# Attention of a hybrid trunk layer: scores of the next group of queries ahead of a group's products, shorter filling, a third P buffer for a weight buffer

## The chip, the cores and the metric

The kernel runs on one core of a Trainium2 chip. The metric is the device time of one execution in microseconds (us). A core has a matrix engine (PE), whose weight loads are listed apart (PEld), a vector engine (DVE), an activation engine (ACT), GpSimd (POOL), and SP, which here only issues DMAs. PE accumulates in PSUM, and the vector and activation engines read results from there.

## What is computed

Two trunk layers over 640 tokens of width 1024 (512 latent tokens, then 128 prompt tokens). Each layer normalises its input, projects it, runs three branches side by side (gated linear attention, latent attention with 4 heads, a diagonal state space model called S5), merges them by sigmoid gates, and projects out. The change is in the attention branch.

```python
def block_attention(q, k, v):
    ...
    def one_block(q_blk):
        s = jnp.einsum('bhqd,bhkd->bhqk', q_blk, k).astype(jnp.float32) * scale
        p = jax.nn.softmax(s, axis=-1).astype(v.dtype)
        return jnp.einsum('bhqk,bhkd->bhqd', p, v)
...
    mixed = (g_a * ((o_a * jax.nn.silu(g_gate)) @ p['w_bo_gla'])
             + g_b * ((o_b * jax.nn.silu(m_gate)) @ p['w_bo_mla'])
             + g_c * ((o_c * jax.nn.silu(s_gate)) @ p['w_bo_s5']))
    y = x + gate * (mixed @ p['w_out'])
```

Latent queries see 256 cached and 512 latent keys (6 blocks of 128); prompt queries see the 128 prompt keys alone.

## The kernel before

Values are split into a rounded high part and the rest (`whi`/`wlo`, `vh`/`vl`, `Pth`/`Ptl`), and a product is the sum of three matmuls. Weights arrive by DMA in raw tiles `wraw` of 128x512, of which there are 4; ACT copies the high part (L227) and DVE subtracts (L236). The order on PE is the order of the code; a scheduler sets the order on the other engines.

The heads (`mla_heads`, L1169) run one after the other. A head has three groups of queries: A and B with two blocks of 128 queries against 768 keys, C with one block against 128 keys. For a block, PE writes scores into two PSUM banks of 128x384 (one for C), DVE finds the maximum of each bank (`tensor_reduce`, L1211), joins and negates them, ACT computes two exponentials from the banks into `P` with the row sums, and DVE adds the sums, takes the reciprocal and scales `P`. `out` (L1228) then turns `P` around on PE (transposes, L1236), in three pieces that are split into `Pth` and `Ptl`, and multiplies each with the values; DVE multiplies the result with a gate into `og` (L1253). `load(h+1)` transposes the next head's queries and keys into single-buffered tiles; `values(h+1)` splits the next head's values into `vh` and `vl`.

The tag `bank` has 4 PSUM banks, shared by scores, transposes, products and loads.

To cover chains on ACT and DVE, `fill(n)` puts n steps of other work on PE, taken from a list of generators, `stand`. One step is mostly six 128x320 matmuls of a projection. In the heads that list holds the merging of the S5 branch, alternating with the modulation of this layer (`ada`, which holds one of the 4 banks until it is done and reads `wraw` directly, two tiles a step), and then early gate tiles of another branch (`mer_early`). `FM` says how many steps stand where: by its places, ahead of A's scores, ahead of A's products, after each piece of products, after B's scores, ahead of B's products, between A's two blocks, between B's two blocks, within C, and within `load`. When the list is empty `fill` puts nothing. Gate tiles not started in the heads are computed in `merge(0, ...)`, near the layer's end, instead of being read back.

Of the kernel before, what the change touches and what calls it, by code (L numbers as in the profile page):

```python
# [10 lines left out]
F32 = mybir.dt.float32  # L11
# [3 lines left out]
AF = mybir.ActivationFunctionType  # L15
ALU = mybir.AluOpType
AX = mybir.AxisListType
# [165 lines left out]


FILL = (17, 2, 1, 4, 2, 10, 10, 1, 7, 3)
FM = (1, 6, 1, 4, 2, 4, 3, 2, 1)
FG = (7, 2, 2, 5, 5)
TCARGS = dict(schedule_with_timeline_sim=True)
OUTS = {"yT": (8, 128, NT), "ckvo": (L, 2, 128, NP_), "kro": (L, 32, NP_), "glao": (L, 4, 128, 128), "s5o": (L, 128, 64)}
# [12 lines left out]
class Prog:  # L202
# [59 lines left out]
        return hi, lo  # L262

    def raw(self, l, name, i):
        r = self.wp.tile([128, 512], F32, name="wraw", tag="wraw", bufs=4)
        self.S.dma_start(r, self.a["wpk"][l, self.at[name]][:, 512 * i:512 * i + 512])
        return r

# [900 lines left out]
    def mla_heads(self, p):  # L1169
        V, fill = self.V, self.fill  # L1170
        scale = 96.0 ** -0.5
        mk = lambda nm, n, b: p.tile([128, n], F32R, name=nm, tag=nm, bufs=b)

        A, B, C = (0, 256, 0, 6), (256, 256, 0, 6), (512, 128, 6, 1)

        def load(h):

            q, k = (mk("qTh", NT, 1), mk("qTl", NT, 1)), (mk("kTh", 896, 1), mk("kTl", 896, 1))
            for src, tiles, d, c0 in ((self.qt, range(0, 4), q, 0), (self.kt, range(0, 4), k, 0),
                                      (self.kt, range(4, 7), k, 512), (self.qt, range(4, 5), q, 512)):  # L1180
                ps = self.bank()
                for i, t in enumerate(tiles):
                    self.T.transpose(ps[0:96, 128 * i:128 * i + 128], src[:, t, h, :], self.ident)
                n = 128 * len(tiles)
                self.split(d[0][0:96, c0:c0 + n], d[1][0:96, c0:c0 + n], ps[0:96, 0:n])
                if c0 == 0 and d is k:
                    fill(FM[8])
            return q, k

        def values(h):  # L1190
            v = [p.tile([128, 7, 128], F32R, name=nm, tag=nm, bufs=1) for nm in ("vh", "vl")]
            self.split(v[0], v[1], self.vt[:, :, 128 * h:128 * h + 128])
            return v

        def scores(qk, grp, n):

            q0, nq, k0, nk = grp
            q, k = qk
            pr = []
            for qi in range(nq // 128):  # L1200
                fill(n * qi)
                qc = slice(q0 + 128 * qi, q0 + 128 * qi + 128)
                P = p.tile([128, 768], F32, name="P", tag="P", bufs=2) if nk > 1 else p.tile([128, 128], F32, name="Pp", tag="Pp")
                mx = p.tile([128, 4], F32, name="smx", tag="smx", bufs=3)
                parts = [(0, 384), (384, 384)] if nk == 6 else [(0, 128)]
                pss = []
                for i, (c0, w) in enumerate(parts):
                    ps = self.bank()
                    kc = slice(128 * k0 + c0, 128 * k0 + c0 + w)
                    self.mm3([ps[:, 0:w]], (q[0][0:96, qc], q[1][0:96, qc]), (k[0][0:96], k[1][0:96]), [kc], True, True)  # L1210
                    V.tensor_reduce(mx[:, i:i + 1], ps[:, 0:w], axis=AX.X, op=ALU.max)  # L1211
                    pss.append(ps)
                if len(parts) == 2:
                    V.tensor_tensor(mx[:, 0:1], mx[:, 0:1], mx[:, 1:2], op=ALU.max)
                V.tensor_scalar(mx[:, 0:1], mx[:, 0:1], -scale, None, op0=ALU.mult)  # L1215
                for i, (c0, w) in enumerate(parts):
                    self.act(P[:, c0:c0 + w], pss[i][:, 0:w], AF.Exp, scale=scale, bias=mx[:, 0:1],
                             accum_out=mx[:, 2 + i:3 + i])
                if len(parts) == 2:
                    V.tensor_tensor(mx[:, 2:3], mx[:, 2:3], mx[:, 3:4], op=ALU.add)  # L1220
                V.reciprocal(mx[:, 2:3], mx[:, 2:3])
                V.tensor_scalar(P[:, 0:128 * nk], P[:, 0:128 * nk], mx[:, 2:3], 0.5, op0=ALU.mult, op1=ALU.mult)
                pr.append(P)
            return pr

        def out(h, pr, v, grp, og, g):
            q0, nq, k0, nk = grp
            po = self.bank()  # L1228
            todo = []
            for k2 in range(0, nk, 2):  # L1230
                ks = range(k2, min(k2 + 2, nk))
                pt = self.bank()
                n = nq * len(ks)
                for i, k in enumerate(ks):
                    for qi in range(nq // 128):
                        self.T.transpose(pt[:, nq * i + 128 * qi:nq * i + 128 * qi + 128], pr[qi][:, 128 * k:128 * k + 128], self.ident)  # L1236
                if nk == 1:
                    th, tl = p.tile([128, 128], F32, name="Pt", tag="Pt", bufs=2), None
                    self.copy(th, pt[:, 0:n])
                else:  # L1240
                    th, tl = mk("Pth", 512, 2), mk("Ptl", 512, 2)
                    self.split(th[:, 0:n], tl[:, 0:n], pt[:, 0:n])
                todo.append((ks, th, tl))
                if len(todo) == 2:
                    yield
                    self.pv(po, v, todo.pop(0), grp)
            yield
            if nk == 1:
                self.mm(po[:, 0:nq], self.vt[:, k0, 128 * h:128 * h + 128], todo[0][1])
            else:  # L1250
                self.pv(po, v, todo.pop(0), grp)
            c = slice(q0, q0 + nq)
            V.tensor_tensor(og[:, c], po[:, 0:nq], g[:, c], op=ALU.mult)  # L1253

        qk, v = load(0), None
        ogs = []
        for h in range(4):
            og = self.ogp.tile([128, NT], F32, name="og", tag="og", bufs=12)
            g = self.gate_in(h)
            fill(FM[0])  # L1260
            pr = scores(qk, A, FM[5])
            if not h:
                v = values(0)
            fill(FM[1])
            for _ in out(h, pr, v, A, og, g):
                fill(FM[2])
            pr = scores(qk, B, FM[6])
            fill(FM[3])
            prc = scores(qk, C, 0)
            if h < 3:  # L1270
                qk = load(h + 1)
            fill(FM[4])
            for _ in out(h, pr, v, B, og, g):
                fill(FM[2])
            for _ in out(h, prc, v, C, og, g):
                fill(FM[7])
            if h < 3:
                v = values(h + 1)
            ogs.append(og)
        return ogs  # L1280
# [10 lines left out]
    def gla_in(self, pa, p):  # L1291
        V, l = self.V, self.l
        self.gq, self.gk = [], []
        for name, dst, s in (("gq", self.gq, 0.125), ("gk", self.gk, 1.0)):
            for i in range(2):
# [3 lines left out]
                dst.append(t)  # L1299
        raw = p.tile([96, 512], F32, name="wa2")  # L1300
        self.S.dma_start(raw, self.a["wa2"][l])
        wa = p.tile([96, 512], F32R, name="wa3")
        self.copy(wa, raw)
        V.tensor_tensor(wa[32:64], raw[32:64], wa[32:64].bitcast(F32), op=ALU.subtract)
        ba = p.tile([128, 512], F32, name="ba")
# [140 lines left out]
    def fill(self, n):  # L1446

        for _ in range(n):
            while self.stand:
                try:  # L1450
                    next(self.stand[0])
                    break
                except StopIteration:
                    self.stand.pop(0)
# [179 lines left out]
```

## Time and profile before

| | |
|---|---|
| time, median of 3 runs | 1606.06 us (1602.31 to 1606.08) |
| profiled execution | 1601.22 us, span 1599.4 us |
| mean granted PE clock | 0.981 |
| busy: PE, DVE, ACT | 95%, 66%, 40% of the span |
| heads of the first layer | about 396 to 540 us of the span |
| heads of the second layer | end at 1328.6 us |

Times in the rows below are us from the span's start. A number in square brackets at a row's end is how long the engine stood idle before that row's first instruction, and what released it.

### The profile page before, as it was taken

What the parts mean: (1) busy time and instruction counts of PE and PEld (TensorE: products, weight loads), DVE (VectorE), ACT (ScalarE), POOL (GpSimd) and SP (SyncE); (2) the same over time, 40 slices, a digit from 0 to 9 for tenths busy, and PEclk for the clock granted to TensorE, in tenths of its full rate; (3) what the DMA queues carried; (4) which work ended last, traced back from release to release, by engine and by line L of the source; (5) the groups of instructions that cost most, each with busy time, mean ns of one, the idle gap of its engine ahead of it and who ended that gap; (6) DMA issues with size and microseconds to landing.
All of it is one profiled execution on the core that took longest, in us unless ns stands there. A gap on an engine that the chain in (4) does not pass through costs nothing. (4 is left out here: it accounts for less than half of the span.)

```text
span 1599.4 us, 28779 instructions
## 1 busy us (share of the span) xinstructions
PE 1516.4 (95%) x11334; PEld 1438.9 (90%) x11334; DVE 1056.4 (66%) x2435; ACT 631.8 (40%) x1171; POOL 47.7 (3%) x48
## 2 busy tenths in 40 slices
PE   4999999999998898999799999999999989989999
PEld 3789999999997888898697999999999979889998
DVE  8986992367566436879987579724766663477762
ACT  3335223555444353333223542244544442634331
POOL 0000000012000000000000000000210000000000
PEclk9999999999999899999899999999999999999999
DMA  9451435323311121227553432442332122212253
GB/s 339 169 152 42 154 114 157 117 86 115 113 55 58 46 75 54 65 85 255 206 193 92 124 112 90 138 151 76 106 120 93 55 66 66 68 60 60 93 166 107
DMA packets 108792, 179.73 MB, mean 112 GB/s; under 512 B 12656, under 2 KB 30768, under 8 KB 108656
## 3 DMA queue, kind: packets, MB, share of 16 engines
q1 hardware_dynamic: 108656, 177.89, 34.3%
q8 instruction: 89, 1.46, 0.4%
q14 instruction: 47, 0.39, 0.1%
HBM read 149.23 MB, written 28.61 MB: 111 GB/s over the span
## 5 line engine op out<-in xcount | busy, mean ns | idle before, releaser
L245 PE MATMUL pj<-h,whi 128*128 128x320 f32 x3456 | 664.1, 313 | 0.0
L245 PEld LDWEIGHTS pj<-h,whi 128*128 128x128 f32 x3456 | 541.2, 189 | 6.6 <-issue 5.1
L227 ACT ACTIVATE whi<-wraw 128x512 fp32r<-128x512 f32 x326 | 205.0, 631 | 508.4 <-PE pj L245 359.2
L245 PE MATMUL pj<-h,wlo 128*128 128x320 f32 x1728 | 397.3, 310 | 0.0
L236 DVE TENSOR_TENSOR wlo<-wraw,whi 128x512 fp32r<-128x512 f32 x326 | 223.9, 688 | 245.5 <-ACT whi L227 238.6
L245 PEld LDWEIGHTS pj<-h,wlo 128*128 128x128 f32 x1728 | 290.3, 188 | 0.0
L245 PE MATMUL pj<-og,whi 128*128 128x320 f32 x736 | 142.1, 313 | 0.3 <-DVE og L236 0.3
L245 PEld LDWEIGHTS pj<-og,whi 128*128 128x128 f32 x736 | 114.7, 188 | 4.7 <-ACT whi L227 1.6
L245 PE MATMUL pj<-whi,h 128*128 128x512 f32 x256 | 87.1, 401 | 6.3 <-ACT h L230 5.7
L245 PE MATMUL pj<-og,wlo 128*128 128x320 f32 x384 | 87.5, 309 | 0.0
L245 PEld LDWEIGHTS pj<-whi,h 128*128 128x128 f32 x256 | 48.7, 192 | 19.5 <-ACT h L230 6.3
L245 PEld LDWEIGHTS pj<-og,wlo 128*128 128x128 f32 x384 | 64.2, 188 | 0.0
L230 ACT ACTIVATE P<-bank,smx 128x384 f32<-128x384 f32 x64 | 36.4, 575 | 56.0 <-DVE smx L1215 56.0
L236 DVE TENSOR_TENSOR Ptl<-bank,Pth 128x512 fp32r<-128x512 f32 x48 | 32.1, 689 | 34.3 <-ACT Pth L227 33.7
L230 ACT ACTIVATE th<-pj 128x640 f32<-128x640 f32 x72 | 49.6, 689 | 5.5 <-PE pj L245 5.4
L245 PE MATMUL pj<-wlo,h 128*128 128x512 f32 x128 | 50.8, 397 | 0.0
L245 PE MATMUL pj<-s5g,whi 128*128 128x320 f32 x256 | 48.1, 310 | 0.0
L245 PE MATMUL bank<-s5qy,mx 128*80 128x128 f32 x256 | 46.1, 302 | 0.0
L227 ACT ACTIVATE Pth<-bank 128x512 fp32r<-128x512 f32 x48 | 27.5, 596 | 41.3 <-PE bank L1236 41.1
L1236 PE MATMUL bank<-c,P 128*128 128x128 f32 x192 | 32.2, 304 | 11.9 <-ACT P L230 5.3
L1211 DVE TENSOR_REDUCE smx<-bank 128x1 f32<-128x384 f32 (+1 forms) x72 | 36.2, 524 | 9.0 <-PE bank L245 8.1
L1400 DVE SCALAR_TENSOR_TENSOR st<-st,bl,bank 64x128 f32<-64x128 f32 x112 | 38.9, 347 | 3.6
(349 smaller groups left out, 2324.2 us busy)
## 6 DMA issues: line engine op xcount, KB each, us to landing
wraw<-wpk SPq DMA_DIRECT2D x358, 256.0 KB, 2.7
og<-wpk SPq DMA_DIRECT2D x48, 256.0 KB, 5.1
qd<-s5qk SPq DMA_DIRECT2D x32, 256.0 KB, 2.2
s5qy<-qd SPq DMA_DIRECT2D x32, 256.0 KB, 4.1
gd<-gt SPq DMA_DIRECT2D x16, 320.0 KB, 2.5
gt<-gd SPq DMA_DIRECT2D x16, 320.0 KB, 3.1
md<-th SPq DMA_DIRECT2D x16, 320.0 KB, 2.3
th<-md SPq DMA_DIRECT2D x16, 320.0 KB, 3.1
```

Source lines behind the costliest of these rows:

```text
L227: self.A.activation(out, in_, AF.Copy, scale=scale)
L230: self.A.activation(out, in_, f, **kw)
L236: (eng or self.V).tensor_tensor(lo, src, hi.bitcast(F32), op=ALU.subtract)
L245: self.T.matmul(out, lhsT, rhs, start=start, stop=stop, skip_group_check=True, **kw)
L1211: V.tensor_reduce(mx[:, i:i + 1], ps[:, 0:w], axis=AX.X, op=ALU.max)
L1236: self.T.transpose(pt[:, nq * i + 128 * qi:nq * i + 128 * qi + 128], pr[qi][:, 128 * k:128 * k + 128], self.ident)
L1400: V.scalar_tensor_tensor(out, st[r, c, :], bl[r, c:c + 1], pu[c][r], op0=ALU.mult, op1=ALU.add)
```

## The change

The function for a group's scores becomes one for a single block of queries, and the loop over heads is written in another order: A's scores of the first head come ahead of the loop; B's first block comes ahead of A's products; B's second block and C come after A's products; and A's two blocks of the next head come ahead of C's product. No filling stands between two blocks of one group. A head without `load` asks for 28 filling steps before and 13 now (4, three times 1, 2, three times 1, 1); `load` adds one in both. `P` gets a third buffer of 128x768, and `wraw` loses one of four.

```diff
-FM = (1, 6, 1, 4, 2, 4, 3, 2, 1)
+FM = (1, 4, 1, 2, 1, 0, 0, 0, 1)
...
-        r = self.wp.tile([128, 512], F32, name="wraw", tag="wraw", bufs=4)
+        r = self.wp.tile([128, 512], F32, name="wraw", tag="wraw", bufs=3)
...
-        def scores(qk, grp, n):
+        def score(qk, grp, qi):
...
-            for qi in range(nq // 128):
-                fill(n * qi)
...
-                P = p.tile([128, 768], F32, name="P", tag="P", bufs=2) if nk > 1 else p.tile([128, 128], F32, name="Pp", tag="Pp")
+            P = p.tile([128, 768], F32, name="P", tag="P", bufs=3) if nk > 1 else p.tile([128, 128], F32, name="Pp", tag="Pp")
...
-        qk, v = load(0), None
+        qk = load(0)
+        fill(FM[0])
+        pa = [score(qk, A, 0), score(qk, A, 1)]
+        v = values(0)
...
-            fill(FM[0])
-            pr = scores(qk, A, FM[5])
-            if not h:
-                v = values(0)
+            pb = [score(qk, B, 0)]
             fill(FM[1])
-            for _ in out(h, pr, v, A, og, g):
+            for _ in out(h, pa, v, A, og, g):
                 fill(FM[2])
-            pr = scores(qk, B, FM[6])
-            fill(FM[3])
-            prc = scores(qk, C, 0)
+            pb.append(score(qk, B, 1))
+            pc = [score(qk, C, 0)]
             if h < 3:
                 qk = load(h + 1)
-            fill(FM[4])
-            for _ in out(h, pr, v, B, og, g):
+            fill(FM[3])
+            for _ in out(h, pb, v, B, og, g):
                 fill(FM[2])
-            for _ in out(h, prc, v, C, og, g):
-                fill(FM[7])
+            if h < 3:
+                pa = [score(qk, A, 0), score(qk, A, 1)]
+            for _ in out(h, pc, v, C, og, g):
+                fill(FM[4])
```

On PE, where the second head of the first layer ends and the third begins, the order was this (`bank<-c,Pp` turns C's block of probabilities around, `pj<-` rows are filling, `bank<-Pt,vt` is C's product, and `bank<-kTh,qTh` begins one part of the scores):

```order
L1236 MATMUL bank<-c,Pp 128x128
L245 MATMUL pj<-h,whi 128x320 x4
L245 MATMUL pj<-h,wlo 128x320 x2
L245 MATMUL pj<-h,whi 128x320 x4
L245 MATMUL pj<-h,wlo 128x320 x2
L245 MATMUL bank<-Pt,vt 128x128
L245 MATMUL pj<-h,whi 128x320 x4
L245 MATMUL pj<-h,wlo 128x320 x2
L245 MATMUL bank<-kTh,qTh 128x384
L245 MATMUL bank<-kTl,qTh 128x384
L245 MATMUL bank<-kTh,qTl 128x384
```

Now the four parts of A stand right behind B's products, and these rows, on the same engine and at the same place, begin with the last of the four (`L389` is the end of the modulation `ada`):

```order
L245 MATMUL bank<-kTh,qTh 128x384
L245 MATMUL bank<-kTl,qTh 128x384
L245 MATMUL bank<-kTh,qTl 128x384
L1232 MATMUL bank<-c,Pp 128x128
L245 MATMUL pj<-og,whi 128x320 x2
L245 MATMUL pj<-tmp,whi 128x320 x2
L245 MATMUL pj<-og,wlo 128x320 x2
L389 MATMUL bank<-c,tmp 128x128 x2
L245 MATMUL bank<-Pt,vt 128x128
L245 MATMUL bank<-kTh,qTh 128x384
L245 MATMUL bank<-kTl,qTh 128x384
L245 MATMUL bank<-kTh,qTl 128x384
```

A's scores moved ahead of C's transposition, without filling between their parts, and B's first block follows C's product at once.

On DVE at that place, the order before was (`smx` is the small tile of maxima and sums, `smx<-bank` a maximum; in both, the first row is the gate product of B):

```order
L1253 TENSOR_TENSOR og<-bank,gt 128x256
L236 TENSOR_TENSOR vl<-vt,vh 128x896
L236 TENSOR_TENSOR wlo<-wraw,whi 128x512
L1253 TENSOR_TENSOR og<-bank,gt 128x128
L1211 TENSOR_REDUCE smx<-bank 128x1 x2
L1214 TENSOR_TENSOR smx<-smx 128x1
L1215 TENSOR_SCALAR smx<-smx 128x1
```

On DVE now:

```order
L1249 TENSOR_TENSOR og<-bank,gt 128x256
L1208 TENSOR_REDUCE smx<-bank 128x1 x2
L236 TENSOR_TENSOR vl<-vt,vh 128x896
L1208 TENSOR_REDUCE smx<-bank 128x1
L1211 TENSOR_TENSOR smx<-smx 128x1
L1208 TENSOR_REDUCE smx<-bank 128x1
L1212 TENSOR_SCALAR smx<-smx 128x1
L1211 TENSOR_TENSOR smx<-smx 128x1
L1212 TENSOR_SCALAR smx<-smx 128x1
```

The split of the values and the two maxima of A's second block now stand between the first block's maxima and its negation (the first L1212), on which its exponentials wait.

The last place is DVE at the boundary between the layers, where the next layer's S5 tables (`s5pw`, `s5w`, `cm`) are prepared beside the output projection of this one (L574). The rows before:

```order
L591 TENSOR_TENSOR cm_8159<-s5pw 128x256
L574 SCALAR_TENSOR_TENSOR mx<-pj,ada_5141,tmp 128x320
L574 SCALAR_TENSOR_TENSOR mx<-pj,ada_5141,tmp 128x192
L574 SCALAR_TENSOR_TENSOR mx<-pj,ada_5141,tmp 128x128
L236 TENSOR_TENSOR wlo<-wraw,whi 128x512
L592 TENSOR_TENSOR s5pw<-cm_8158,cm_8159 128x4x64
```

The rows on DVE there now:

```order
L592 TENSOR_TENSOR s5w<-cm_8105,cm_8106 128x8x64
L596 TENSOR_TENSOR cm_8110<-s5pw,s5sm 128x512
L597 TENSOR_TENSOR cm_8111<-s5pw,s5sm 128x512
L236 TENSOR_TENSOR h<-mx,h 128x640
L236 TENSOR_TENSOR wlo<-wraw,whi 128x512
L708 TENSOR_SCALAR s5pw<-s5pw,c 128x8x64
L598 TENSOR_TENSOR s5w<-cm_8110,cm_8111 128x8x64
L709 TENSOR_SCALAR s5pw<-s5pw 128x8x64
L574 SCALAR_TENSOR_TENSOR mx<-pj,ada_5402,tmp 128x320
```

The part of the tables from `s5pw<-cm, 128x4x64` up to L709, 14 instructions, moved from behind the first output tile to ahead of it. In this order one gate tile fewer is computed in the first layer's heads, and three fewer in the second's; they stand in `merge(0, ...)` now.

## Rows read from the trace of the kernel before

**Rows 1.** The page's first part: busy us (share of the span) xinstructions, by engine.

```profile
PE 1516.4 (95%) x11334; PEld 1438.9 (90%) x11334; DVE 1056.4 (66%) x2435; ACT 631.8 (40%) x1171; POOL 47.7 (3%) x48
```

**Rows 2.** Table by windows: heads with filling and without it, both layers.

```profile
core 0: us, PE busy (x) PEld busy (x) DVE busy (x) ACT busy (x) POOL busy (x), PEclk, DMA share, GB/s
400.00:500.00 100.00, 100.00 (x721) 97.00 (x721) 60.52 (x146) 43.04 (x99) 0.00 (x0) 1.00 0.25 81
499.84:540.31 40.47, 27.46 (x146) 22.49 (x145) 26.07 (x70) 19.04 (x49) 0.00 (x0) 0.83 0.11 35
1200.00:1300.00 100.00, 100.00 (x719) 98.66 (x718) 62.73 (x151) 46.29 (x107) 0.00 (x0) 1.00 0.24 75
1302.07:1328.60 26.53, 17.43 (x87) 15.04 (x85) 15.71 (x42) 12.03 (x30) 0.00 (x0) 0.74 0.14 41
```

**Rows 3.** Timeline of PE, first layer: start us, us, instruction, [idle before <-releaser].

```profile
499.84 0.34 PE L245 MATMUL bank<-kTh,qTh 96*128 96x384 f32 x1
...
517.64 0.30 PE L1236 MATMUL bank<-c,P 128*128 128x128 f32 x1 [3.12 <-ACT P L230]
...
530.06 0.48 PE L245 MATMUL bank<-kTh,qTh 96*128 96x128 f32 x1 [3.56 <-ACT P L230]
```

**Rows 4.** Timeline of PE, second layer.

```profile
1302.07 0.34 PE L245 MATMUL bank<-kTh,qTh 96*128 96x384 f32 x1
...
1318.54 0.48 PE L245 MATMUL bank<-kTh,qTh 96*128 96x128 f32 x1 [3.56 <-ACT P L230]
```

**Rows 5.** Timeline of PE in a head with filling, first layer.

```profile
448.54 0.75 PE L245 MATMUL pj<-h,whi 128*128 128x320 f32 x4
...
449.42 0.75 PE L245 MATMUL pj<-h,whi 128*128 128x320 f32 x4
...
452.94 1.03 PE L1236 MATMUL bank<-c,P 128*128 128x128 f32 x8
453.73 0.54 PE L245 MATMUL pj<-og,whi 128*128 128x320 f32 x2
...
459.02 0.34 PE L245 MATMUL bank<-kTh,qTh 96*128 96x384 f32 x1
```

**Rows 6.** Instructions on tile smx, 400 to 540 us: min/median/max ns.

```profile
L1211 DVE TENSOR_REDUCE smx<-bank x36: 292/551/559, 401.6 to 531.0; 128x1 f32<-128x384 f32 x32, 128x1 f32<-128x128 f32 x4
L230 ACT ACTIVATE P<-bank,smx x32: 562/573/585, 404.3 to 531.0; 128x384 f32<-128x384 f32 x32
L1222 DVE TENSOR_SCALAR P<-P,smx x16: 610/620/623, 406.0 to 532.5; 128x768 f32<-128x768 f32 x16
```

**Rows 7.** Timeline of PE, DVE and ACT where A's blocks follow each other without filling.

```profile
511.75 1.09 DVE L236 TENSOR_TENSOR vl<-vt,vh 128x896 fp32r<-128x896 f32 x1 [0.56 <-ACT vh L227]
...
512.18 0.42 PE L245 MATMUL bank<-kTh,qTh 96*128 96x384 f32 x1
...
514.18 0.34 PE L245 MATMUL bank<-kTh,qTl 96*128 96x384 f32 x1
...
515.21 0.58 ACT L230 ACTIVATE P<-bank,smx 128x384 f32<-128x384 f32 x1 [3.33 <-DVE smx L1215]
```

**Rows 8.** Table by windows of low granted clock (columns as in Rows 2).

```profile
529.00:539.20 10.20, 7.26 (x32) 6.54 (x33) 4.77 (x17) 4.50 (x13) 0.00 (x0) 0.51 0.14 45
1317.40:1327.70 10.30, 7.62 (x33) 6.91 (x34) 5.00 (x17) 4.61 (x13) 0.00 (x0) 0.51 0.18 46
```

**Rows 9.** Layer boundary: timeline of PE, then the window (columns as in Rows 2).

```profile
800.16 0.58 PE L245 MATMUL bank<-s5qk,s5rd 128*32 128x112 f32 x2 [12.20 <-DVE s5qk L718]
...
770.00:810.00 40.00, 27.80 (x197) 27.16 (x196) 39.34 (x76) 7.41 (x12) 0.00 (x0) 0.83 0.47 162
```

**Rows 10.** Weights: the page's split on DVE; SP's waits (us, times, longest); DMA landing.

```profile
L236 DVE TENSOR_TENSOR wlo<-wraw,whi 128x512 fp32r<-128x512 f32 x326 | 223.9, 688 | 245.5 <-ACT whi L227 238.6
...
SPq L266 <- DVE wlo L236: 654.4, 214, 9.0
...
wraw<-wpk SPq DMA_DIRECT2D x358, 256.0 KB, 2.7
```

More of the change, by code (lines that the diff above doesn't have):

```diff
@@ L1193, in values @@
             return v
-        def scores(qk, grp, n):
+        def score(qk, grp, qi):
             q0, nq, k0, nk = grp
             q, k = qk
-            pr = []
-            for qi in range(nq // 128):
-                fill(n * qi)
-                qc = slice(q0 + 128 * qi, q0 + 128 * qi + 128)
-                P = p.tile([128, 768], F32, name="P", tag="P", bufs=2) if nk > 1 else p.tile([128, 128], F32, name="Pp", tag="Pp")
[L1204 to L1224, printed above, removed]
@@ new lines, in score @@
+            qc = slice(q0 + 128 * qi, q0 + 128 * qi + 128)
+            P = p.tile([128, 768], F32, name="P", tag="P", bufs=3) if nk > 1 else p.tile([128, 128], F32, name="Pp", tag="Pp")
+            mx = p.tile([128, 4], F32, name="smx", tag="smx", bufs=3)
+            parts = [(0, 384), (384, 384)] if nk == 6 else [(0, 128)]
+            pss = []
+            for i, (c0, w) in enumerate(parts):
+                ps = self.bank()
+                kc = slice(128 * k0 + c0, 128 * k0 + c0 + w)
+                self.mm3([ps[:, 0:w]], (q[0][0:96, qc], q[1][0:96, qc]), (k[0][0:96], k[1][0:96]), [kc], True, True)
+                V.tensor_reduce(mx[:, i:i + 1], ps[:, 0:w], axis=AX.X, op=ALU.max)
+                pss.append(ps)
@@ new lines, in score @@
+            if len(parts) == 2:
+                V.tensor_tensor(mx[:, 0:1], mx[:, 0:1], mx[:, 1:2], op=ALU.max)
+            V.tensor_scalar(mx[:, 0:1], mx[:, 0:1], -scale, None, op0=ALU.mult)
+            for i, (c0, w) in enumerate(parts):
+                self.act(P[:, c0:c0 + w], pss[i][:, 0:w], AF.Exp, scale=scale, bias=mx[:, 0:1],
+                         accum_out=mx[:, 2 + i:3 + i])
+            if len(parts) == 2:
+                V.tensor_tensor(mx[:, 2:3], mx[:, 2:3], mx[:, 3:4], op=ALU.add)
@@ L1226, in out @@
+            V.reciprocal(mx[:, 2:3], mx[:, 2:3])
+            V.tensor_scalar(P[:, 0:128 * nk], P[:, 0:128 * nk], mx[:, 2:3], 0.5, op0=ALU.mult, op1=ALU.mult)
+            return P
         def out(h, pr, v, grp, og, g):
```

## The prediction

> **What bounds the kernel now.** I read the busy shares first. PE works 1516.4 us of the span, ACT 631.8, DVE 1056.4 [rows 1]; so PE's queue sets the time, and only time in which PE idles or runs at a low clock can be won. The table by windows then shows where that is in the heads. While filling lasts, PE is busy 100.00 us of 100 and the granted clock is 1.00, in both layers; when it has run out, the clock is 0.83 and 0.74 and a third of each window is idle [rows 2]. The timeline gives the points: in layer 0 the last filling ends at 499.84, between B's two blocks of the third head, and in layer 1 at 1302.07, between A's two blocks of the fourth [rows 3, 4]. Behind these points the idles are P's chain, up to 3.56 us at a time. Another place matters for the change: at the boundary between the layers PE stands 12.20 us for DVE's tables, with DVE busy 39.34 us of 40 around it [rows 9].
>
> **What the two tails cost.** Their work at the high clock is worked out from the filled head. A filling step is 0.88 us (448.54 to 449.42). A group's transposes and products with three steps between them run from 452.94 to 459.02, 6.08 us; less 3 x 0.88 that is 3.44 [rows 5]. Four parts of scores take from 512.18 to 514.18 and the start of the next matmul, 2.1 us, so 1.05 a block [rows 7]. Eight transposes take 0.79 us [rows 5], so a load's twelve 1.2. C's scores and product I estimate at 0.55, from matmuls a third as wide. Layer 0's tail holds five blocks (5.25), three groups (10.3), one load and two C (2.3): 17.9 of 40.47 us, so 22.6 are lost. Layer 1's holds three blocks, two groups and one C: 10.6 of 26.53, so 15.9. Together 38.5 us. Of that, half of PE's busy time in the stretches at 0.51, (7.26 + 7.62) / 2 = 7.4 us, is the clock's [rows 8]. 1.2 GHz is the lower level, and it was entered behind idles of 3.12 and 3.56 us [rows 3, 4].
>
> **What is removed.** A head takes 29 filling steps before and 14 after (28 and 13 in the last), with two ahead of the first head: 57 a layer. Layer 0 has some 75: of the 100 us to 500 [rows 2] about 2.5 heads of attention at 12.9 us (four blocks, two groups, a load and C) take 32, and the other 68 hold 77 steps of 0.88, some of them `ada`'s shorter ones. Layer 1's lasts a head longer. So the filling no longer runs out, and both tails go: **-38.5 us**. What filling is left runs behind the heads, at the same price a step.
>
> **What is added: stalls within the heads.** The two blocks of A now stand back to back, and what PE does next waits for PSUM banks. Take the third head's entry in the order printed above, from the start of A's scores. Where the same pair ran without filling, its first exponential began 3.03 us after the scores did (512.18 to 515.21), with the split of the values, 1.09 us, ahead of the maxima [rows 7]. Now that split stands behind two of the maxima and ahead of the negation, so I add it: 4.1 us. The exponential takes 0.57 [rows 6], so a bank comes free at 4.7. PE has finished four parts at 2.1, and needs the bank for C's transposition: 2.6 us idle. Then it fills for one step, and C's product waits until ACT, behind four exponentials (4.1 + 4 x 0.57 = 6.4), has copied `Pt`: another 1.0. With queueing on DVE **3.6 us**; the fourth head's entry has the same order, 3.6. At the second head's entry `ada` still holds one bank. There the fourth part waits for the first exponential already (1.6 to 4.7, 3.1 us), and C's transposition and B's two parts each for one more release, 1.8 together: **4.9**. The first head puts A and B's first block in a row on three banks: 3.7 by the same steps without the split of values, and 2.4 in its load, whose transposes wait for C's exponential and one more. The loads of the second and third heads wait about 1.0 each, with four banks. In the last head B's products wait for the scaled P: a block's chain is 1.05 of scores, 0.55 for the last maximum, two exponentials, 0.62 for the scaling [rows 6] and some 1.0 of small steps, 4.4 us, of which C's scores and two steps hide 2.1, and at the block's place in the queue some more: 1.8. The layer's sum is 6.1 + 4.9 + 3.6 + 3.6 + 2.0 + 1.8 = 22.0, **+44 us** for two.
>
> Bounds: if DVE reached the negation as early as in [rows 7], three entries would save 1.1 each, and the first head about 1: -9 us. If one more split of 0.69 us [rows 10] stood ahead at each of the eight entries and the first load, +6. DVE makes this possible: 60.52 of 100 us now [rows 2], but a head that drops from 29 to 14 steps is about half as long and holds the same softmax work, so DVE comes near to full.
>
> At this step a rule can be weighed against the rows. With filling between all parts and the same four banks the trace shows no idle at all [rows 2]. By the Trainium skill, "Perfetto Trace Analysis", section "Optimization Strategy", the same gap repeating on the engine that should be saturated can mean that there is not enough PSUM for the next tile. By the rows alone there would be no stalls and the sum would be -44; by the rule they recur in every head, as walked above, and no run here shows that yet.
>
> **The clock.** Idles of 3.12 and 3.56 us were followed by a stretch at 1.2 GHz [rows 3, 8]; the new ones are 2.6 to 3.1 with 1 to 2 us more close behind. Ahead of and behind them stands dense work. A fall of 3.4 us costs half of it, 1.7. I take about two and a half in eight entries: **+4 us**, between 0 and 8 x 1.7 = 14.
>
> **The boundary.** The gate tile moved out of layer 0's heads is computed ahead of the output projection: eight steps, 7.0 us of PE, in which DVE can work on the tables of the next layer; the order shows 14 of its instructions moved ahead of the first output tile. PE's 12.20 us of idle [rows 9] shrink by at most 7.0; DVE spends 2 x 0.69 on the tile's weights [rows 10], so I take **-5.6**, between 0 and -7. The three tiles moved in layer 1 are the same work elsewhere: 0.
>
> **The buffers.** SP's queue stands 654.4 us for `wlo` to free a raw buffer, and a weight lands 2.7 us after its issue [rows 10]: the queue runs ahead of need, so one buffer fewer costs 0 as long as two tiles per 8 steps (7.0 us) are wanted, against 2.7 + 0.63 + 0.69 for one. What could uncover it is `ada`, with two tiles a step: if each of its eight steps waited 0.6 us, 5 us a layer. I take 0. The third `P` is what lets B's block be scored while A's two are in use; at 0 it removes no wait of before, since scores then waited on nothing in the filled windows.
>
> **Sum.** -38.5 + 44 + 4 - 5.6 = **+3.9 us**. The profiled execution took 1601.22, 4.8 under the median of 1606.06; I put the sum on the middle of the two and the range of runs, 1603.9: **1608 us**. What a measurement here can tell from no change is about 0.3%, 4.8 us.
>
> **Rivals.**
> *The stalls are half of the walk (faster).* If ACT and DVE reach the exponentials early at every entry and the bank releases fall under C's scores and the fill step, 44 becomes 22 and the clock term 0: -22, **1582 us**. For it: the third and fourth heads have four banks. Against it: the printed order puts the split of the values ahead of the negation, and ACT is in order. It decides from 35 us of stall in two layers downward.
> *The clock falls at every entry (slower).* Eight falls of 3.4 us and stretches like those at 0.51, which lasted 10 us [rows 8], where two waits lie close together: the clock term 4 becomes 16, **1620 us**. It decides if more than five of eight entries fall. The Trainium skill, "TensorE: Matmul & The Clock Gate", section "HAM oscillation — how this bites in real kernels", tells of such a kernel, which fell back to half rate in every round of a loop. By it the time is this rival's; the rows of before, with one fall for each long idle, neither exclude nor demand it.
> *Weights come late with three buffers (slower).* `ada` takes two of three, the filling beside it waits for its tile behind them in SP's order: 5 us a layer, **1618 us**. Against it is the 654.4 us of waiting in SP's queue.
> *The change trades place only.* Stalls equal the tails and nothing happens at the boundary: inside the forecast's own range.
>
> **How the numbers follow.** Forecast 0.52, own range 1599 to 1617 (its stall bounds -9 and +6, boundary and a part of the clock); half stalls 0.25; clock at every entry 0.14; late weights 0.09. The range 1588 to 1620 leaves a tenth below, among the half-stall cases, and a tenth above. Faster: 0.25 and an eighth of the forecast, 0.32. Slower: 0.14 + 0.08 and a third of the forecast, 0.40. Same: 0.28.
>
> **What would show it.** Right: no stretch in the heads without filling matmuls; idles of 2 to 3.5 us on PE in front of C's transposition in the third and fourth heads, released by ACT's P, and 1 us for `Pt`; PE busy about 80% in the heads; PE's idle at the boundary 5 to 8 us. Wrong: heads at PE 95% (then the walk of DVE is at fault), clock under 0.9 through all heads, or PE or ACT waiting on `wraw`.

## The result, and the profile after

The changed kernel takes 1620.28 us (median of 4 runs, 1617.79 to 1622.56) against 1606.07 before: a ratio of 1.0093, 95% interval 1.0073 to 1.0113. It is 14 us slower, where 1608 was forecast; the time lies just above the range. Run again, beside other kernels, it was 1618.37 against 1603.58, 1.0090 (1.0074 to 1.0107). The profiled execution took 1622.52 us, the long end of its runs, and that of before, 1601.22, the short end of all runs of that kernel (1600.4 to 1610.9); so the two profiles are 21 us apart, some 7 more than the medians.

The page's first part, busy us by engine, answers to [rows 1]:

```profile
PE 1530.4 (94%) x11334; PEld 1449.5 (89%) x11334; DVE 1056.6 (65%) x2435; ACT 631.7 (39%) x1171; POOL 47.0 (3%) x48
```

The number of matmuls is the same, and PE's busy time is 14.0 us longer. Most of that is the clock: in tables by windows of 2 us, busy time times one less the granted clock adds up to 34.3 us over the whole span, against 21.5 before, 12.8 more. PE's idle time grew by 7.3. To find where, I cut both spans at the same points of the program: the first transposes of a layer's heads, the first cumulative sum of the linear attention behind them, and the start of the next layer's S5 products. The table by windows of after, for the stretch ahead of the heads, the heads with what is left of the filling, the second layer up to its heads, and its heads (columns as in [rows 2]):

```profile
0.00:401.30 401.30, 374.38 (x2868) 353.64 (x2869) 286.18 (x703) 160.50 (x284) 17.08 (x19) 0.99 0.45 143
401.30:602.70 201.40, 183.89 (x1155) 170.94 (x1153) 106.52 (x242) 87.61 (x182) 1.24 (x3) 0.94 0.22 66
805.60:1186.20 380.60, 378.37 (x2834) 362.85 (x2835) 251.39 (x549) 153.23 (x274) 18.15 (x15) 0.98 0.40 121
1186.20:1385.60 199.40, 181.23 (x1153) 168.22 (x1151) 106.93 (x242) 88.14 (x183) 1.24 (x3) 0.96 0.22 67
```

The same four stretches of before:

```profile
0.00:397.50 397.50, 372.24 (x2869) 352.36 (x2870) 286.46 (x704) 160.77 (x284) 18.07 (x19) 0.99 0.44 145
397.50:597.40 199.90, 186.80 (x1203) 173.24 (x1200) 106.96 (x243) 88.93 (x184) 1.24 (x3) 0.97 0.22 71
800.20:1177.60 377.40, 375.12 (x2834) 360.47 (x2835) 251.33 (x550) 154.46 (x274) 17.80 (x15) 0.99 0.39 121
1177.60:1385.70 208.10, 198.80 (x1299) 187.44 (x1297) 109.95 (x247) 92.55 (x190) 1.24 (x3) 0.97 0.24 76
```

Idle time is a stretch less PE's busy time: in the two heads' stretches 13.1 and 9.3 us before, 17.5 and 18.2 after. What the low clock costs I take from the same table cut in pieces of 2 us, busy time times one less the granted clock: 5.0 and 5.2 before, 10.8 and 8.0 after. Together 32.6 before and 54.5 after: **the heads lost 22 us**. (Their stretches do not show it as length, since a gate tile in the first layer and three in the second, 7.0 us each, now stand behind them: the records show 48 and 146 matmuls fewer.) The stretches ahead of the heads, which the new order of the loop does not touch, are longer by **3.8 and 3.2 us**; in the second, 3.1 of the 3.2 are low clock (7.1 us against 4.1).

The idles of the first layer's heads, in the timeline of PE, the longest at each place (the number in square brackets):

```profile
408.60 0.44 PE L245 MATMUL bank<-kTh,qTh 96*128 96x384 f32 x1 [1.61 <-ACT P L230]
410.12 0.44 PE L245 MATMUL bank<-kTh,qTh 96*128 96x384 f32 x1 [0.71 <-ACT P L230]
411.84 0.69 PE L245 MATMUL bank<-kTh,qTh 96*128 96x384 f32 x1 [0.93 <-ACT P L230]
428.20 0.64 PE L1183 MATMUL bank<-c,qt 128*96 128x128 f32 x4 [1.24 <-ACT Pp L230]
444.61 0.44 PE L245 MATMUL bank<-kTh,qTh 96*128 96x384 f32 x1 [3.15 <-ACT P L230]
463.41 0.64 PE L1183 MATMUL bank<-c,kt 128*96 128x128 f32 x4 [1.03 <-ACT Pp L230]
477.94 0.33 PE L1232 MATMUL bank<-c,Pp 128*128 128x128 f32 x1 [2.36 <-ACT P L230]
510.87 0.47 PE L1232 MATMUL bank<-c,Pp 128*128 128x128 f32 x1 [2.36 <-ACT P L230]
530.54 0.95 PE L1232 MATMUL bank<-c,P 128*128 128x128 f32 x7 [1.59 <-DVE P L1219]
```

These are the waits that the prediction walked, one by one, most of them for PSUM banks; the idles of 3.12 and 3.56 us in the old tails [rows 3, 4] are gone. What it did not see coming is in the windows right behind the four entries:

```profile
412.00:416.00 4.00, 4.00 (x15) 4.00 (x16) 2.50 (x8) 1.52 (x5) 0.00 (x0) 0.50 0.19 45
446.00:448.00 2.00, 2.00 (x9) 1.80 (x8) 1.80 (x7) 1.74 (x6) 0.00 (x0) 0.50 0.00 0
480.00:486.00 6.00, 6.00 (x22) 6.00 (x23) 4.25 (x17) 1.49 (x5) 0.00 (x0) 0.50 0.34 100
512.00:516.00 4.00, 4.00 (x15) 3.82 (x15) 2.74 (x7) 0.67 (x3) 0.00 (x0) 0.50 0.26 69
```

The granted clock is 0.50, 1.2 GHz, behind every one, with PE busy throughout. In the second layer it was low behind all four entries too:

```profile
1198.20:1200.20 2.00, 2.00 (x8) 2.00 (x8) 1.67 (x5) 0.63 (x1) 0.00 (x0) 0.50 0.04 8
1230.20:1232.20 2.00, 2.00 (x8) 1.90 (x9) 1.09 (x5) 1.05 (x4) 0.00 (x0) 0.50 0.30 111
1264.20:1266.20 2.00, 2.00 (x11) 1.90 (x10) 1.41 (x4) 2.00 (x8) 0.00 (x0) 0.53 0.00 0
1296.20:1298.20 2.00, 2.00 (x8) 1.75 (x8) 1.50 (x5) 0.50 (x3) 0.00 (x0) 0.50 0.00 0
```

One idle of 2.36 us stood ahead of the fall in the fourth head, and a sequence of 1.61, 0.71 and 0.93 at the first entry.

At the boundary of the layers the idle of [rows 9] has shrunk to 4.39 us:

```profile
805.58 0.58 PE L245 MATMUL bank<-s5qk,s5rd 128*32 128x112 f32 x2 [4.39 <-DVE s5qk L718]
```

### The profile page after: what moved, and what is told of

The parts are those of the page before. It is cut to its first block, busy times and chain, and to the rows that moved or that the text cites. A ratio compares the mean times of both kernels' runs of the same rounds, so it can differ in the third digit from the quotient of the medians.

```text
span 1620.7 us, 28764 instructions
## 1 busy us (share of the span) xinstructions
PE 1530.4 (94%) x11334; PEld 1449.5 (89%) x11334; DVE 1056.6 (65%) x2435; ACT 631.7 (39%) x1171; POOL 47.0 (3%) x48
## 5 line engine op out<-in xcount | busy, mean ns | idle before, releaser
L245 PE MATMUL pj<-og,whi 128*128 128x320 f32 x736 | 147.1, 321 | 0.3 <-DVE og L236 0.3
L245 PEld LDWEIGHTS pj<-og,whi 128*128 128x128 f32 x736 | 118.6, 195 | 4.8 <-ACT whi L227 1.6
L245 PEld LDWEIGHTS pj<-s5g,whi 128*128 128x128 f32 x256 | 41.2, 193 | 0.0
```

The lines of the kernel that those rows point to most:

```text
L245: self.T.matmul(out, lhsT, rhs, start=start, stop=stop, skip_group_check=True, **kw)
```

## The experiments

The theory: the four entries let the clock fall in each head, and this, more than the waits, is the loss; the raw buffer costs nothing. The rivals: the waits alone; the raw buffer; the shorter filling in itself. All intervals are 95%. Idle and low-clock losses of the heads are for both layers, read as above.

**Three raw buffers alone.** The kernel before, with one edit.

```diff
-        r = self.wp.tile([128, 512], F32, name="wraw", tag="wraw", bufs=4)
+        r = self.wp.tile([128, 512], F32, name="wraw", tag="wraw", bufs=3)
```

> The kernel before with three raw weight buffers and nothing else. Clock theory (the loss of the change is the granted clock that falls to 1.2 GHz behind the new waits at the four head entries of each layer): the buffer costs nothing, within 3 us of before, about 1606. Rival, buffers (a raw weight comes late): it carries most of the loss, 1612 to 1620.

Measured: 1616.99 us against 1606.66, 1.0065 (1.0044 to 1.0086). The rival is right here: the buffer alone costs 10 us. Most of it does not lie in the heads. The windows ahead of both layers' heads (columns as before):

```profile
0.00:405.50 405.50, 377.41 (x2868) 356.18 (x2869) 285.94 (x702) 159.70 (x284) 21.13 (x19) 0.98 0.45 141
809.80:1189.50 379.70, 375.38 (x2834) 360.31 (x2835) 250.78 (x548) 153.09 (x273) 18.33 (x15) 0.99 0.40 120
```

They are 8.0 and 2.3 us longer than in the kernel before. Over all the profiles of this study the stretch ahead of the first heads takes 397.2 to 400.9 us with four buffers (7 profiles, mean 398.6) and 401.3 to 405.5 with three (7 profiles, mean 403.4); the second 375.0 to 380.2 (mean 377.5) and 377.7 to 381.2 (mean 379.9). So some 7 us of it lie there, by the means; the ranges of the second stretch overlap, and only the first's 5 us are clear.

**More work in the gaps.** The changed kernel, with 14 more matmuls at each entry, whose results nobody reads (`gap` is part 0 of A's second block in the first two heads and part 1 in the others):

```diff
+                if i == gap:
+                    more = self.pj.tile([128, 2, 512], F32, name="pj", tag="pj")
+                    for _ in range(14):
+                        self.mm(more[:, 0, :320], q[0][0:96, 0:128], k[0][0:96, 0:320])
...
-                pa = [score(qk, A, 0), score(qk, A, 1)]
+                pa = [score(qk, A, 0), score(qk, A, 1, int(h > 0))]
```

> The changed kernel with 14 more matmuls of 128x320 (about 2.1 us at 2.4 GHz) on PE at each entry to a head, in a spare PSUM tile that nobody reads, in the place where PE waited 2.4 to 3.2 us. It does more work and takes nothing away from the chain that PE waits for. Clock theory: the idles shrink under 1.2 us, the clock stays at 2.4 GHz, and 10 to 16 of the 19 us at the low clock come back: 1604 to 1610. Rival, waits alone (the chain's length is the loss, the clock a side show): 1620 to 1626, since the added work only replaces idle time or adds to it.

Measured: 1618.28 us, 1.0071 (1.0044 to 1.0098); against the changed kernel's 1.0093 no clear difference. The heads' stretches:

```profile
403.80:600.60 196.80, 183.87 (x1211) 171.30 (x1208) 106.11 (x242) 87.96 (x183) 1.24 (x3) 0.99 0.23 68
1184.80:1381.30 196.50, 183.90 (x1211) 171.33 (x1209) 105.92 (x242) 87.98 (x183) 1.24 (x3) 0.99 0.22 68
```

The clock stayed up, but for one fall at the first head of each layer: its loss went from 18.8 us to 3.4, 15 back, as the clock theory said, and the two stretches are 7.5 us shorter although PE executes 8 x 14 matmuls more, 16.4 us at the 0.88 / 6 of a filling step [rows 5]. Idle fell only from 35.7 to 25.5, so 6 us of the added work were no cover but length. My expectation had put all of it into idle time. The mechanism held in the heads; the total, 8 us above the expected range, did not.

**Filling between A's blocks.** The changed kernel with the same number of steps, three of them elsewhere.

```diff
-FM = (1, 4, 1, 2, 1, 0, 0, 0, 1)
+FM = (1, 1, 1, 2, 1, 0, 0, 3, 1)
...
-                pa = [score(qk, A, 0), score(qk, A, 1)]
+                pa = [score(qk, A, 0)]
+                fill(FM[7])
+                pa.append(score(qk, A, 1))
```

(The first head's pair, ahead of the loop, likewise.)

> The changed kernel with three of the four filling steps that stood behind B's first block moved between A's two blocks, so that a head has as many steps as in the changed kernel. Clock theory: the waits at the entries (3.2, 3.15, 2.4, 2.4 us a layer) mostly go and with them the falls of the clock; A's products wait 1 to 2 us for the second block's P instead: 20 to 28 us under the changed kernel, 1592 to 1600. Waits alone: about 10 to 12 us, 1608 to 1610. Buffers: no gain beyond 3 us.

Measured: 1601.55 us, 0.9966 of before (0.9950 to 0.9981), 19 us under the changed kernel, just short of the 20 to 28 expected. The heads' stretches are 11.3 and 10.0 shorter than after:

```profile
403.70:593.80 190.10, 176.11 (x1153) 162.63 (x1151) 105.06 (x242) 87.87 (x182) 1.24 (x3) 0.99 0.23 70
1178.80:1368.20 189.40, 176.31 (x1155) 162.13 (x1153) 105.17 (x242) 88.68 (x183) 1.24 (x3) 0.99 0.23 70
```

The low clock costs 3.0 us in both together, idle 27.1. So 15.8 us of low clock and 8.6 of idle are gone, 3 more than the stretches got shorter, which isn't explained. The shorter waits alone are under half of what the stretches lost.

**The values' low part on GpSimd.** The changed kernel, with `vl` off DVE.

```diff
-            self.split(v[0], v[1], self.vt[:, :, 128 * h:128 * h + 128])
+            self.split(v[0], v[1], self.vt[:, :, 128 * h:128 * h + 128], eng=self.G)
```

> The changed kernel with the low part of the values (vl, 1.09 us on DVE) computed on GpSimd, so that it no longer stands between the maxima and the negation at an entry. If the split is what makes the waits long (my walk: 1.1 us at each of three entries a layer), waits of 1.3 us in the third and fourth heads and 2.0 in the second, 6 to 7 us less in all, and where a shorter wait no longer lowers the clock up to 8 more: 1606 to 1614. If the bank order holds the entry anyway: 1620. GpSimd's own time for the split is not known from the trace; above 4 us the products of A would wait for it.

Measured: 1618.31 us, 1.0084 (1.0052 to 1.0115): no gain to be told. The timeline of all engines at the third head's entry shows why:

```profile
476.88 2.10 POOL L236 TENSOR_TENSOR vl<-vt,vh 128x896 fp32r<-128x896 f32 x1 [31.74 <-ACT vh L227]
...
477.85 1.14 DVE L1211 TENSOR_TENSOR smx<-smx 128x1 f32<-128x1 f32 x1
...
480.28 0.33 PE L1232 MATMUL bank<-c,Pp 128*128 128x128 f32 x1 [2.41 <-ACT P L230]
```

The joining of two maxima, an instruction on one element per partition that takes 0.15 us elsewhere, took 1.14 and ended with GpSimd's instruction (478.98). PE's wait is 2.41 us, as long as with the split on DVE. At the fourth head's entry the same instruction took 1.14 us again. So the run says nothing on how much the split's place costs: DVE stood still for about as long as it had worked before.

**The old order with shorter filling.** The kernel before with 18 steps a head where there were 29 (`load`'s step counted in both), and four raw buffers.

```diff
-FM = (1, 6, 1, 4, 2, 4, 3, 2, 1)
+FM = (1, 3, 1, 2, 1, 2, 1, 1, 1)
```

> The kernel before, its order and its buffers, with shorter filling alone: FM (1, 3, 1, 2, 1, 2, 1, 1, 1), 18 steps a head where there were 28. If the short filling in itself is what costs (chains uncovered in every head), slower than before by 5 or more: over 1611. If the loss of the change sits in its order of scores and in the buffer, this keeps the clock up and loses only the tails: 32.7 us of idle and low clock in the two layers' heads shrink to 10 to 20, 1590 to 1600.

Measured: 1594.73 us, 0.9949 (0.9932 to 0.9966). Short filling is no loss, it is a gain: idle and low clock in the heads are 25.1 us (23.7 and 1.4) where they were 32.6 before. The expectation had 10 to 20 there. By the two ratios this kernel is 23 us under the changed one, so the loss lies in the new order and its buffers, not in short filling as such.

**Four raw buffers in the changed kernel.** The room is taken from `Ptl`.

```diff
-        r = self.wp.tile([128, 512], F32, name="wraw", tag="wraw", bufs=3)
+        r = self.wp.tile([128, 512], F32, name="wraw", tag="wraw", bufs=4)
...
-                    th, tl = mk("Pth", 512, 2), mk("Ptl", 512, 2)
+                    th, tl = mk("Pth", 512, 2), mk("Ptl", 512, 1)
```

> The changed kernel with four raw weight buffers again; the room comes from Ptl, which goes from two buffers to one. Two causes side by side: the raw buffer carries about 10 us (as three buffers in the kernel before did), so 1608 to 1612, first heads at about 397 us as before. Clock alone: 1618 to 1622.

Measured: 1619.51 us, 1.0108 (1.0090 to 1.0127). No gain, against the expectation. The stretch ahead of the second layer's heads was 377.1 us, that of the old kernel, but the heads were 1.7 and 1.4 us longer, which is less than two profiles of one kernel can differ by (201.4 and 197.8 us for the changed kernel's first heads). Whether `Ptl` ate what the buffer gave took three more runs on one chip: the changed kernel as it is, again with four buffers and one `Ptl`, and with three and one.

> The changed kernel as it is, beside the next two on one chip, since the run with four raw buffers and one Ptl took as long as the changed kernel did on another day: 1616 to 1622.

> The changed kernel with four raw buffers and one Ptl. If the raw buffer costs as the stages before the heads say (5 us ahead of the first heads, 3 in the second layer), 5 to 9 us under the changed kernel run beside it, less what one Ptl costs. If the buffer's cost belongs to the old kernel alone: the same time.

> The changed kernel with one Ptl and three raw buffers: the price of the room that the fourth raw buffer took. From the heads of the profiled runs, 201.4 and 199.4 us with two and 203.1 and 200.8 with one, it costs 3 us over the changed kernel; if nothing, the heads agree within 1 us.

Measured, in this order: 1618.37 (1.0090; 1.0074 to 1.0107), 1618.19 (1.0089; 1.0069 to 1.0109) and 1624.30 us (1.0116; 1.0096 to 1.0135). By these medians one `Ptl` would cost 6 us, and the fourth raw buffer give the same 6 back; but the three intervals overlap, so neither is shown. The price of one `Ptl` isn't seen in the profiled execution of that kernel either (1617.38 us, the shortest of its six runs).

**Both repairs.** The filling between A's blocks, with four raw buffers and one `Ptl`.

> Both repairs together: three of the filling steps between A's two blocks, and four raw weight buffers with one of Ptl. If the two causes add up, 1590 to 1594 (the run with the filling moved, 1601.6, less 8 to 10). If the buffer's cost was another's, 1600.

Measured: 1591.80 us, 0.9935 (0.9914 to 0.9957), in the expected stretch. But the kernel before ran at 1602.25 us beside this one and at 1606.66 beside the run with the filling moved: against it the two kernels won 10.5 and 5.1 us, so the buffers are worth some 5 us here, not 10, and the intervals of the ratios meet. That the two causes simply add up isn't shown.

**Three more steps a head.** The run before, with

```diff
-FM = (1, 1, 1, 2, 1, 0, 0, 3, 1)
+FM = (1, 2, 1, 2, 1, 1, 0, 4, 1)
...
             pc = [score(qk, C, 0)]
+            fill(FM[5])
             if h < 3:
                 qk = load(h + 1)
```

> As the run before, with three more filling steps a head, out of what is left over behind the heads: one ahead of A's products, one more between A's blocks, one ahead of the load, where its transposes waited 1.0 us. Waits left in the heads were 14 and 13 us; half of them go: 1583 to 1589. If the waits left are DVE's, which has more to split per step, no gain: 1590 to 1594.

Measured: 1588.47 us, 0.9908 (0.9890 to 0.9926), in the expected range; the interval overlaps that of the run before. The heads' idle went from 24.6 to 17.2. This order starts all eight gate tiles of the first layer in the heads again, and the boundary's idle is back at 13.41 us. The last run makes the first layer stop at seven:

```diff
-        for j in range(8):
+        for j in range(8 if self.l else 7):
```

> The kernel with more filling and four raw buffers (1588.5 us), with one early gate tile fewer in the first layer, so that it is computed ahead of the output projection. If a tile there gives DVE time for the next layer's tables, PE's idle at the boundary falls from 13.4 us to 4 to 6 and 6 to 8 us are won: 1580 to 1583. If the idle depends on something else, no change.

Measured: 1585.86 us, 0.9889 (0.9873 to 0.9905). The idle at the boundary, timeline of PE, with eight tiles and with seven:

```profile
789.88 0.58 PE L245 MATMUL bank<-s5qk,s5rd 128*32 128x112 f32 x2 [13.41 <-DVE s5qk L718]
...
790.69 0.58 PE L245 MATMUL bank<-s5qk,s5rd 128*32 128x112 f32 x2 [4.00 <-DVE s5qk L718]
```

It fell as expected, from 13.41 to 4.00, but the total by 2.6 us and not by 6 to 8, and the intervals overlap. In the profiled executions the heads without that tile were 2.0 us shorter instead of 7.0, with 2.9 more of low clock and 1.4 more idle. Why isn't settled: the two profiled executions are the shortest run of the one (1584.87) and the longest of the other (1589.00). Both kernels beat the old and the changed one.

## Why the prediction was wrong, step by step

**What bounds the kernel**: right. PE's idle and its clock make the difference, in the heads and over the whole span.

**What the two tails cost**: 38.5 us forecast, 32.6 measured by idle and clock in the stretches of before; the term was too large by 6. In the windows of [rows 2] PE was busy for 44.9 us, of which the low clock is 10.0, so the tails' work took 34.9 us at the high clock where the working had 28.5. My reading is that transposes and products without filling between them overlap less; that was not measured.

**Stalls within the heads**: 44 us forecast, 35.7 measured (17.5 and 18.2). The places and their releasers were right; the sizes were right or walked too long, by some half at three places. Entry by entry, first layer: 3.7 walked, 1.61 + 0.71 + 0.93 = 3.25 measured; the first load 2.4 and 1.24 + 0.35; the second head 4.9 and 3.15; the third 3.6 and 2.36 + 0.43; the fourth 3.6 and 2.36; loads 1.0 and 1.03; the last head 1.8 and 1.59. The exponential that was walked to start 4.1 us behind A's scores started 3.9 behind them. This timeline of after, of DVE, ACT and PE, shows the chain of the third head, whose scores began at 473.30:

```profile
475.03 1.08 DVE L236 TENSOR_TENSOR vl<-vt,vh 128x896 fp32r<-128x896 f32 x1
...
477.04 0.14 DVE L1212 TENSOR_SCALAR smx<-smx 128x1 f32<-128x1 f32 x1
...
477.21 0.58 ACT L230 ACTIVATE P<-bank,smx 128x384 f32<-128x384 f32 x1 [2.76 <-DVE smx L1212]
...
479.45 0.29 ACT L227 ACTIVATE Pt<-bank 128x128 f32<-128x128 f32 x1
```

The split stands where the printed order put it, and the copy of `Pt` waits behind four exponentials. One sign named in the prediction did not show: PE was to be busy for about 80% of the heads, and was for 111.81 us of the 129.24 from the first load to the last wait of the first layer's heads, 87%. DVE, which the walk's upper bound had near full there, was busy for 79.74 us, 62%.

**The clock**: this step failed, and by the most. The prediction took two and a half falls in eight entries, at 1.7 us each, +4 us; there were eight of eight, at 1.5 to 3.2 us each, 2.4 in the mean. A fall of 3.4 us, the length it was priced at, stands in the trace of before (518.5 to 521.9); four of the new ones lasted some 6.8. The heads' low-clock loss is 18.8 us in the profile after; it was 10.2 in the tails before, which were counted within the 38.5. The trace of before had a warning that the prediction passed over, since it read only the idles of 3.12 and 3.56 us. In the second layer's tail two shorter ones stood close together, and the clock fell to 0.50 at the second (1307.0 to 1310.4):

```profile
1305.52 0.30 PE L1236 MATMUL bank<-c,P 128*128 128x128 f32 x1 [2.22 <-ACT P L230]
1307.23 1.73 PE L1236 MATMUL bank<-c,P 128*128 128x128 f32 x7 [1.41 <-DVE P L1222]
```

The rival "The clock falls at every entry", 1620 us, had 0.14, and its mechanism came true. That its time did too is in part luck: it holds nothing for the buffer, and its other terms were off in ways that nearly cancel. By the Trainium skill, "TensorE: Matmul & The Clock Gate", section "HAM oscillation — how this bites in real kernels", a wait in each round of a loop makes PE pay the transition in each round; this trace agrees, with 0.50 behind all four entries. The run with more work in the gaps shows that the idle of the entries does it: more matmuls, 15 us less of low-clock loss.

**The buffers**: this step failed too. "the queue runs ahead of need, so one buffer fewer costs 0" was argued from 654.4 us of SP's waiting [rows 10]. Alone it costs 10 us in the old kernel, and by the medians 6 in the changed one (1624.30 to 1618.19, both with one `Ptl`, intervals that overlap), most of it ahead of the heads, which the prediction didn't look at, since it argued from the heads' filling and `ada`. The sum over the queue was no evidence for each stage. Which transfer is late there wasn't followed: with three buffers the other engines' order there differs as well.

**The boundary**: -5.6 forecast, 12.20 to 4.39 measured, -7.8. The mechanism was right, and the size a little over its bound of 7.0; in a second profile of the changed kernel the idle is 5.55, -6.7, within it.

**The sum.** Measured by stages between the two profiles: heads +21.9, boundary -7.8, stretches ahead of the heads +7.0, together +21.1 of the 21.3 between the spans; the forecast had +9.5, -5.6 and 0. Smaller stalls (-8) and smaller tails (+6) nearly cancel; the clock (+15) and the stretches ahead of the heads (+7) are what is missing. Of the 7, the 3.2 of the second layer are low clock and need not be the buffer's: in a second profile of the changed kernel (span 1616.4) that stretch took 377.7 us, 0.3 over before, and the first one 403.7, 6.2 over. The heads' loss is there again, 51.9 us against 32.6. Against the medians, 14 us apart, the first profile overstates the loss by 7, and from which stage that comes isn't known. What the third `P` buffer is worth by itself was not run.

**The rules.** The gap that repeats on the engine that should be saturated, from the Trainium skill, "Perfetto Trace Analysis", section "Optimization Strategy", was a matter of PSUM here, as that rule allows: each of the entry's longer waits ends with an exponential that frees a bank. No run had more banks; filling between the blocks mended it without one.

## What to carry to other kernels

Where a chain on slower engines is put further ahead, put the filling into the place where the leading engine now waits for buffers, not behind it: the same 14 steps a head, three of them elsewhere, were worth 19 us. Price a wait that recurs by the clock that it loses as well as by its length. A buffer given away is paid for in other stages than the one that got it; try it alone.

## What the runs showed of the hardware that was not expected

An idle of 2.36 us between stretches of dense matmuls was followed by 0.50 of the clock for 3 to 7 us. Shorter idles sometimes were and sometimes were not: in the run with filling between A's blocks, whose heads lost 3.0 us in two layers, an idle of 2.09 us stood at the first entry of both layers, and the clock fell behind it only in the second. A line of PE's timeline there, then a window (columns as in [rows 2]):

```profile
1191.35 0.45 PE L245 MATMUL bank<-kTh,qTh 96*128 96x384 f32 x1 [2.09 <-ACT P L230]
...
1192.80:1194.80 2.00, 2.00 (x13) 0.86 (x13) 1.97 (x5) 0.00 (x0) 0.00 (x0) 0.50 0.14 28
```

The clock also fell where PE showed no idle at all: in the changed kernel behind 20 matmuls of 128x1, 2.29 us from 1107.23, and in the kernel before not behind the same 20 (1101.10). A DVE instruction on one element per partition lasted 1.14 us instead of 0.15 beside a GpSimd subtraction of 128x896, and ended with it. By the Trainium skill, "Perfetto Trace Analysis", section "Optimizing Scalar/DVE Operations", the two share a read port to SBUF, so moving work from one to the other might not help; the run agrees.
